# Two-tile transfers of the expert weights, with the kept results and the sample states laid out anew

## The chip, the cores and the metric

The kernel runs on one core of a Trainium2 chip. The metric is the device time of one execution in microseconds; the times below are the median and the ends of several runs. The trace is one profiled execution of the same program.

## The reference

One inference step of a two-layer decoder for 512 prompt tokens and 8 sample sequences of 4 tokens (544 rows of 1024). Each layer is a mixer and a product-key expert block (PEER):

```python
h = rmsnorm(x, g_mix); proj = h @ w_in                  # pool, q/k/v, z, beta, alpha, xq, 3 gates
y = [pool_mixer(...), gated_delta(...), mem_attend(...)]  # the delta branch carries a state per sequence
x = x + sum_n(sigmoid(gate_n) * (y_n @ w_branch[n])) @ w_o
h = rmsnorm(x, g_ffn)
s = subkeys . (h @ w_q)          # 8 heads, 2 halves, 128 keys each: top 16 of each, then top 16 of the sums
a = einsum('td,thed->the', h, take(U, idx))            # 16384 experts, 8 x 16 chosen per token
x = x + einsum('the,thed->td', softmax(best) * gelu(a), take(V, idx))
```

The outputs are the normed rows and the new pool, convolution, delta and memory states.

## The kernel before

Matrix products run as three float32r products of a high and a low part: a helper `split` (lines 94 to 96) makes the high part on ACT (`wh`, `vh`) and the low part on DVE (`wl`, `vl`), and TensorE takes high x high, high x low and low x high. Raw weight tiles come through `weights` (line 98): one ring named `wr` of three buffers of 4 KB a partition, and two buffers each for `wh` and `wl`. All of `w_mk`, `w_mv`, `w_in`, `w_branch`, `w_o`, `w_pq` and the expert table `u` go through that ring; the loads are issued on SP's queue, in program order.

A layer goes like this. **Mixer**: attention, convolution, pooling, then gates and the delta branch; `delta_sample` (line 719) reads the sample states in four loads of eight sequences (`S0`, two buffers of 4 KB), once for the products and once more to update and store them. **out_proj** (line 322) multiplies by `w_o` in eight tiles for token groups 2, 3, 4 and again in eight for groups 0, 1. **scores** (line 1215) finds the key scores, and loads the first eight expert tiles ahead into buffers of their own (`pre`, PRE = 8). **The G stage** (`second_stage`, `make_g`) turns, for the first 384 tokens (ND), the chosen experts and gates into a dense map of one-hot products; it is work of DVE. Beside it `spend` puts, by estimated costs, dense expert tiles on TensorE (`a_tile`: one tile of `u`, 24 products of 384 columns; 72 tiles before the G stage ends) and gathered rows for the other 160 tokens (`gather`: an indirect DMA of 128 rows on POOL's queue into one of four buffers `g_r`, then one DVE operation, `g_junk` or `g_acc`). The results of the first 24 dense tiles stay in SBUF in `kept` (36 KB a partition), the others go to DRAM (`ad`). **The v loop** (line 1053 on) runs 128 steps; a step multiplies one column tile of the gated results with one tile of `v` (`vr`, ring of three buffers of 4 KB, line 1096; 18 products of 512 columns), and between the steps the remaining 56 tiles of `u` and 200 gathered rows are placed. At steps 20, 24 and 28 the residual rows `xmid` are loaded into a buffer of the same `vr` ring (line 1122) and added on TensorE by the identity.

The program is written in this order, but a list scheduler with a timeline model sets the final order of each engine's and each queue's instructions. SBUF is handed out from two ends: pools open on the left unless `side="right"`. `hx`, the mixer's input and later its merged result, lies on the right; `pre` and then the gather's pool `gp` use the same right end once `hx` is closed after out_proj. `kept` lies in the pool `pe` on the left for the whole expert block.

Of the kernel before, what the change touches and what calls it, by code (L numbers as in the profile page):

```python
# [9 lines left out]
F32 = mybir.dt.float32  # L10
# [7 lines left out]
P = 128  # L18
L = 2
# [6 lines left out]
NB = 8  # L26
# [50 lines left out]
class Body:  # L77
# [20 lines left out]
    def weights(self, src, n=1024, wr=None):  # L98
        nc = self.nc
        if wr is None:  # L100
            wr = self.wp.tile([P, 1024], F32, name="wr", bufs=3)
            nc.sync.dma_start(wr[:, :n], src)
        wh = self.wp.tile([P, 1024], F32R, name="wh", bufs=2)
        wl = self.wp.tile([P, 1024], F32R, name="wl", bufs=2)
        self.split(wh[:, :n], wl[:, :n], wr[:, :n])
        return wh, wl
# [612 lines left out]
    def delta_sample(self, l, dl):  # L719
        nc, a = self.nc, self.a  # L720

        def state(h):
            S0 = dl.tile([P, NB, P], F32, name="S0", bufs=2)
            nc.sync.dma_start(S0, a["state_delta"][l, :, h * NB:(h + 1) * NB])
            return S0
# [9 lines left out]
        for g in range(32):  # L735
            if g % NB == 0:
                S0 = state(g // NB)
            nc.tensor.matmul(ps[:, g], S0[:, g % NB], wq[:, g], start=True, stop=True)
# [18 lines left out]
        for c in range(8):  # L757
            h = c // 2
            if c % 2 == 0:
                S0 = state(h)  # L760
            p = self.bank(1).rearrange("p (b e) -> p b e", b=4)
            for j in range(4):
                b = (c % 2) * 4 + j
                nc.tensor.matmul(p[:, j], kdm[h * 32:(h + 1) * 32, b], vn[h * 32:(h + 1) * 32], start=True, stop=True)
            for j in range(4):
                b = (c % 2) * 4 + j
                g = c * 4 + j
                nc.vector.scalar_tensor_tensor(S0[:, b], S0[:, b], r["egr"][:, 0, g * 4 + 3:g * 4 + 4], p[:, j],
                                               op0=OP.mult, op1=OP.add)
            if c % 2 == 1:  # L770
                nc.sync.dma_start(a["ndelta_s"][l, :, h * NB:(h + 1) * NB], S0)
# [141 lines left out]
    def a_fetch(self):  # L913
        k = self.a_next
        self.a_w = self.weights(self.a["u"][self.a_l, k], wr=self.pre.pop(k, None)) if k < NKEY else None
# [44 lines left out]
    def peer(self, l):  # L960
# [7 lines left out]
        with ExitStack() as es:  # L968
# [6 lines left out]
            self.kept = pe.tile([P, KJ, ND], F32, name="kept")  # L975
# [7 lines left out]
            with ExitStack() as es2:  # L983
# [27 lines left out]
                self.hxs.close()  # L1011
                sc = self.pool("sc", es2)
                pp = self.pool("pre", es2, side="right")
                self.pre = {k: pp.tile([P, D], F32, name=f"pre{k}") for k in range(PRE)}
# [3 lines left out]
                while self.pre:  # L1018
                    self.a_early(len(self.pre) > 1)
# [17 lines left out]
            with ExitStack() as es2:  # L1037
# [23 lines left out]
                def out(i, x, parts):  # L1061
# [3 lines left out]
                    if l + 1 < L:  # L1065
                        self.mixer_in(ns, i, parts, g, 0, h)
                        if x is None:
                            x = acc[1] if i == 4 else dv.tile([P, D], F32, name="vr", bufs=3)
                            x = x[:np_]
                            for s, p in enumerate(parts):  # L1070
                                nc.scalar.copy(x[:, s * 512:(s + 1) * 512], p)
# [4 lines left out]
                for q in order:  # L1076
# [8 lines left out]
                    for jj in range(GA):  # L1085
# [10 lines left out]
                        vr = dv.tile([P, D], F32, name="vr", bufs=3)  # L1096
                        nc.sync.dma_start(vr, a["v"][l].rearrange("(i j) d -> j i d", j=P)[j])
# [22 lines left out]
                        if step % 4 == 0 and XAT <= step < XAT + 4 * (ND // P):  # L1120
                            i = (step - XAT) // 4
                            x = dv.tile([P, D], F32, name="vr", bufs=3)
# [10 lines left out]
                        if step == NKEY - RDONE + 1:  # L1133
                            for _ in self.rows_due:
                                pass
                            ge.close()
                            if l + 1 < L:
# [78 lines left out]
    def scores(self, l, sc, val, idx, bh, bl):  # L1216
# [4 lines left out]
        for h in range(PH):  # L1221
            if h % 4 == 0:
                ssm = sc.tile([P, 2, NKEY], F32, name="ssm", bufs=2)
            for k in list(self.pre)[h * PRE // PH:(h + 1) * PRE // PH]:
# [158 lines left out]
def _layout(inp):  # L1383
# [34 lines left out]
    o["u"] = np.ascontiguousarray(u.transpose(0, 2, 4, 3, 1)).reshape(L, P, P, NK * P)  # L1418
# [82 lines left out]
```

## Time and profile before

| | us |
|---|---|
| runs shown: median (lowest, highest) of 3 | 4025.16 (4023.65, 4027.57) |
| the profiled execution's own time | 4027.84 |
| its span in the trace | 4026.0 |
| TensorE (PE) busy | 3878.3 (96%) |
| VectorE (DVE) busy | 2950.2 (73%) |
| ScalarE (ACT) busy | 1603.4 (40%) |
| mean granted TensorE clock | 0.978 |

The span is what the trace covers; the profiled execution's own time is 1.84 us longer. PE's busy time is the union of matmuls whose ends are modelled, so a full PE is not by itself PE at its peak; the issue distance between matmuls in the chain tells more. The two layers repeat the same pattern at a distance of some 1980 us.

### The profile page before, as it was taken

The page shows a single profiled execution, that of the slowest core. Times are in us where ns is not written, and L with a number is a line of the kernel's source. Part 1 is how long each engine was busy: PE and PEld are TensorE (multiplying, and loading weights), DVE is VectorE, ACT ScalarE, POOL GpSimd, SP SyncE. Part 2 cuts the span into 40 slices and gives each one's busy share as a digit, 9 for nine tenths or more (in the row PEclk, how much of TensorE's full clock was granted, in tenths as well). Part 3 has the DMA queues.
Part 4 walks back from the last instruction along what each step waited for, and adds up shares of the span by engine and source line. Part 5 has one row for each costly group of instructions (what it writes and reads, how often), then busy time and mean ns, then how long its engine had stood idle before and what let it go on. Part 6 is the DMA issues. An engine that isn't in the chain of part 4 may idle for free.

```text
span 4026.0 us, 63148 instructions
## 1 busy us (share of the span) xinstructions
PE 3878.3 (96%) x24116; PEld 3522.3 (87%) x24116; DVE 2950.2 (73%) x5811; ACT 1603.4 (40%) x2373; POOL 1038.8 (26%) x880
## 2 busy tenths in 40 slices
PE   8999999999997999999999999999999889999998
PEld 7899997898996888888888999889989778888887
DVE  5544445789998888888855444467999978888887
ACT  4532333334554333333444333343355543333333
POOL 0110110003323444443401111000034434444443
PEclk9999999999997999999999999999999889999999
DMA  7233114427888999999933322162378899999996
GB/s 261 82 124 120 54 59 149 169 64 243 302 314 317 336 344 345 337 339 339 339 111 117 125 83 67 48 235 86 101 270 302 321 335 332 346 341 342 347 333 238
DMA packets 318272, 917.60 MB, mean 228 GB/s; under 512 B 28400, under 2 KB 109680, under 8 KB 314640
## 3 DMA queue, kind: packets, MB, share of 16 engines
q1 hardware_dynamic: 218896, 518.21, 38.0%
q0 software_dynamic: 92160, 335.59, 23.2%
q10 hardware_dynamic: 6912, 59.77, 3.7%
q8 instruction: 189, 3.10, 0.3%
q14 instruction: 115, 0.94, 0.1%
HBM read 826.19 MB, written 87.26 MB: 227 GB/s over the span
## 4 chain that ended last, share of the span: by engine, by line
PE 85%; DVE 8%; issue 3%; DMA 2%; ACT 2%; POOL 1%; DVEq 0%; POOLq 0%; SPq 0%; ACTq 0%
PE mm L115 31%; PE mm L1113 17%; PE sm L115 12%; PE sm L1113 9%; PE mm L341 2%; DVE wl L96 2%; DMA g_r<-u_rows,g_e 2%; DVE g_junk L1182 1%; PE sm L628 1%; PE sm L616 1%; PE sm L904 1%; PE sm L622 1%; PE sm L885 1%; DVE ohl L1363 1%; PE sm L522 1%
## 5 line engine op out<-in xcount | busy, mean ns | idle before, releaser
L95 ACT CAST wh<-wr 128x1024 fp32r<-128x1024 f32 (+1 forms) x464 | 466.9, 1006 | 1042.8 <-PE mm L115 676.0
L96 DVE TENSOR_TENSOR wl<-wr,wh 128x1024 fp32r<-128x1024 f32 (+1 forms) x464 | 543.3, 1171 | 384.2 <-ACT wh L95 383.5
L1197 POOL DMA_INDIRECT g_r<-u_rows,g_e x320 | 459.4, 1436 | 1374.3 <-DVE g_junk L1182 654.3
L1197 POOL DMA_INDIRECT g_r<-v,g_e x320 | 449.3, 1404 | 553.7 <-DVE g_acc L1190 511.1
L115 PE MATMUL mm<-ah,wh 128*128 128x384 f32 (+1 forms) x1408 | 467.5, 332 | 19.3 <-ACT ga L934 12.6
L115 PE MATMUL mm<-ah,wl 128*128 128x384 f32 (+1 forms) x1408 | 464.2, 332 | 15.0 <-DVE wl L96 14.7
L115 PE MATMUL mm<-al,wh 128*128 128x384 f32 (+1 forms) x1408 | 461.7, 328 | 0.5 <-DVE al L96 0.5
L1190 DVE SCALAR_TENSOR_TENSOR g_acc<-g_r,g_w,g_acc 128x1024 f32<-128x1024 f32 x320 | 409.7, 1280 | 12.3 <-DMA g_r<-v,g_e 10.3
L1182 DVE SCALAR_TENSOR_TENSOR g_junk<-g_r,h2t 128x1024 f16<-128x1024 f32 x320 | 390.0, 1219 | 30.3 <-DMA g_r<-u_rows,g_e 28.9
L96 DVE TENSOR_TENSOR vl<-vr,vh 128x1024 fp32r<-128x1024 f32 x256 | 312.3, 1221 | 38.7 <-ACT vh L95 38.3
L115 PE MATMUL mm<-hh,wh 128*128 128x272 f32 x1536 | 335.4, 295 | 0.2 <-ACT hh L95 0.2
L115 PE MATMUL mm<-hh,wl 128*128 128x272 f32 x1536 | 334.3, 295 | 0.0
L115 PE MATMUL mm<-hl,wh 128*128 128x272 f32 x1536 | 328.0, 293 | 0.0
L1113 PE MATMUL mm<-vl,gwh 128*128 128x512 f32 x1024 | 316.9, 390 | 0.0
L1113 PE MATMUL mm<-vh,gwl 128*128 128x512 f32 x1024 | 316.1, 390 | 0.0
L115 PE MATMUL sm<-ah,wl 128*128 128x384 f32 x896 | 303.5, 339 | 5.9 <-DVE wl L96 5.9
L1113 PE MATMUL mm<-vh,gwh 128*128 128x512 f32 x1024 | 304.1, 392 | 2.2 <-ACT vh L95 2.2
L115 PE MATMUL sm<-ah,wh 128*128 128x384 f32 x896 | 304.7, 340 | 0.7 <-ACT stage L1372 0.7
L115 PE MATMUL sm<-al,wh 128*128 128x384 f32 x896 | 303.6, 339 | 0.0
L115 PEld LDWEIGHTS mm<-ah,wh 128*128 128x128 f32 x1408 | 267.8, 190 | 28.2 <-ACT ga L934 18.8
L115 PEld LDWEIGHTS mm<-ah,wl 128*128 128x128 f32 x1408 | 267.6, 190 | 24.0 <-DVE wl L96 23.7
L95 ACT CAST vh<-vr 128x1024 fp32r<-128x1024 f32 x256 | 269.1, 1053 | 12.1 <-DMA vr<-v 11.4
(436 smaller groups left out, 8133.7 us busy)
## 6 DMA issues: line engine op xcount, KB each, us to landing
vr<-v SPq DMA_DIRECT2D x256, 512.0 KB, 6.9
wr<-u SPq DMA_DIRECT2D x240, 512.0 KB, 6.1
wr<-w_in SPq DMA_DIRECT2D x96, 512.0 KB, 3.6
gd<-stage ACTq DMA_DIRECT2D x24, 1664.0 KB, 8.5
gt<-gd SPq DMA_DIRECT2D x52, 768.0 KB, 10.7
ad<-ga ACTq DMA_DIRECT2D x24, 768.0 KB, 6.4
gr<-ad SPq DMA_DIRECT2D x24, 768.0 KB, 8.3
wr<-w_o SPq DMA_DIRECT2D x32, 512.0 KB, 3.8
```

Source lines behind the costliest of these rows:

```text
L95: self.nc.scalar.copy(hi, src)
L96: self.nc.vector.tensor_sub(lo, src, hi.bitcast(F32))
L115: nc.tensor.matmul(o, w[:, k * P:(k + 1) * P], x[part][:, k], start=(q == 0), stop=(q == 3 * nk - 1))
L341: nc.tensor.matmul(ps[i][s][:np_], m[:, k, c], w[:, s * 512:(s + 1) * 512], start=(k == 0 and q == 0), stop=(k == NK - 1 and q == 2))
L522: nc.tensor.matmul(ps[i], x[:, k, i * P:(i + 1) * P], w[:, kk * BW:(kk + 1) * BW], start=(k == 0 and q == 0), stop=(k == NK - 1 and q == 2))
L616: nc.tensor.matmul(p[:, h], ats[:, h], dm[:, h], start=True, stop=True)
L622: nc.tensor.matmul(p[:, h], dtm[:, h], xm[:, h], start=True, stop=True)
L628: nc.tensor.matmul(p[:, h], xm[:, h], dtm[:, h], start=True, stop=True)
L1113: ins = nc.tensor.matmul(po[i][s], w[:, i * P:(i + 1) * P], v[:, s * 512:(s + 1) * 512], start=(step == 1 and m == 0), stop=(step == NKEY ...
L1182: ins = nc.vector.scalar_tensor_tensor(jk, r, 1.0, h2t[t], op0=OP.mult, op1=OP.mult, accum_out=w[:, s:s + 1])
L1190: nc.vector.scalar_tensor_tensor(acc[t], r, w[:, s:s + 1], acc[t], op0=OP.mult, op1=OP.add)
L1197: nc.gpsimd.indirect_dma_start(out=r, out_offset=None, in_=a["v" if which else "u_rows"].rearrange("l e d -> (l e) d"), in_offset=bass.Ind ...
```

## The change

Three things are done. (1) The host stores two tiles of `u` side by side; a load brings a pair, 8 KB a partition, into a ring `wr` of two buffers of 8 KB in place of three of 4 KB. Other weights still load one tile, into the first half of such a buffer. The `v` tiles are also loaded in pairs, into a ring `vr` of two buffers of 8 KB, which the `xmid` rows share; `pre` becomes four pairs. (2) `kept` is opened on the right end after out_proj, below `pre` and `gp`, and closed near the end of the v loop. (3) The sample states come in pieces of four sequences, with three buffers of 2 KB, and are stored in such pieces.

```diff
     def weights(self, src, n=1024, wr=None):
-            wr = self.wp.tile([P, 1024], F32, name="wr", bufs=3)
+            wr = self.wp.tile([P, 2048], F32, name="wr", bufs=2)
...
-        def state(h):
-            S0 = dl.tile([P, NB, P], F32, name="S0", bufs=2)
-            nc.sync.dma_start(S0, a["state_delta"][l, :, h * NB:(h + 1) * NB])
+        def state(c):
+            S0 = dl.tile([P, 4, P], F32, name="S0", bufs=3)
+            nc.sync.dma_start(S0, a["state_delta"][l, :, c * 4:(c + 1) * 4])
...
-            if c % 2 == 0:
-                S0 = state(h)
+            S0 = state(c)
...
-            if c % 2 == 1:
-                nc.sync.dma_start(a["ndelta_s"][l, :, h * NB:(h + 1) * NB], S0)
+            nc.sync.dma_start(a["ndelta_s"][l, :, c * 4:(c + 1) * 4], S0)
...
     def a_fetch(self):
         k = self.a_next
-        self.a_w = self.weights(self.a["u"][self.a_l, k], wr=self.pre.pop(k, None)) if k < NKEY else None
+        if k == NKEY:
+            self.a_w = None
+            return
+        if k % 2 == 0:
+            self.a_pair = self.pre.pop(k // 2, None)
+            if self.a_pair is None:
+                self.a_pair = self.wp.tile([P, 2048], F32, name="wr", bufs=2)
+                self.nc.sync.dma_start(self.a_pair, self.a["u"][self.a_l, k // 2])
+        self.a_w = self.weights(None, wr=self.a_pair[:, k % 2 * D:(k % 2 + 1) * D])
...
-            self.kept = pe.tile([P, KJ, ND], F32, name="kept")
...
                 self.hxs.close()
+                ke = ExitStack()
+                self.kept = self.pool("kept", ke, side="right").tile([P, KJ, ND], F32, name="kept")
                 sc = self.pool("sc", es2)
                 pp = self.pool("pre", es2, side="right")
-                self.pre = {k: pp.tile([P, D], F32, name=f"pre{k}") for k in range(PRE)}
+                self.pre = {k: pp.tile([P, 2 * D], F32, name=f"pre{k}") for k in range(PRE // 2)}
...
-                        vr = dv.tile([P, D], F32, name="vr", bufs=3)
-                        nc.sync.dma_start(vr, a["v"][l].rearrange("(i j) d -> j i d", j=P)[j])
+                        if jj % 2 == 0:
+                            vp = dv.tile([P, 2 * D], F32, name="vr", bufs=2)
+                            nc.sync.dma_start(vp, a["v"][l].rearrange("(i j n) d -> j i (n d)", j=P // 2, n=2)[j // 2])
+                        vr = vp[:, jj % 2 * D:(jj % 2 + 1) * D]
...
-                            x = dv.tile([P, D], F32, name="vr", bufs=3)
+                            x = dv.tile([P, 2 * D], F32, name="vr", bufs=2)[:, :D]
                             nc.sync.dma_start(x, self.xmid[l][i])
...
                             ge.close()
+                            ke.close()
```

The new sizes and places also move instructions. Two places on SP's queue matter below.

The first is out_proj in layer 0. In the changed program SP's queue reads there (`w_branch`, `w_o` and `w_pq` are weights, `sg` a gate read back, `pre` the expert pairs loaded ahead):

```order
L102 DMA wr<-w_o 128x1024 x2
L1235 DMA pre_7218<-u 128x2048
L1235 DMA pre_7219<-u 128x2048
L1235 DMA pre_7220<-u 128x2048
L1235 DMA pre_7221<-u 128x2048
L102 DMA wr<-w_o 128x1024 x7
L349 DMA xmid_80<-x_o 128x1024 x2
```

and before the same loads stood after the last `w_o` tile and three tiles of `w_pq`:

```order
L102 DMA wr<-w_pq 128x1024 x3
L1225 DMA pre_7195<-u 128x1024
L1225 DMA pre_7196<-u 128x1024
L349 DMA xmid_80<-x_o 128x1024
L1225 DMA pre_7197<-u 128x1024
L1225 DMA pre_7198<-u 128x1024
L349 DMA xmid_80<-x_o 128x1024
L1225 DMA pre_7199<-u 128x1024
```

So the four pairs, 4 MB, have moved ahead of the last twelve `w_o` tiles: `pre` no longer lies where `hx` is still read. Layer 1 has the same order.

The second place is the part of the v loop in which the `xmid` rows use a `vr` buffer. In the changed program SP's queue reads there, with what each row waits for:

```order
L1132 DMA vr<-xmid_80 128x1024 [waits DMAHW4_49,DMAHW2_49,DVE_49]
L1105 DMA vr<-v 128x2048 [waits DMAHW5_49,DMAHW3_49,DVE_49]
L1105 DMA vr<-v 128x2048 [waits DMAHW4_49,PE_49]
L1132 DMA vr<-xmid_80 128x1024 [waits DMAHW5_49,DVE_49]
L920 DMA wr<-u 128x2048 [waits DVE_49,Activation_49]
```

and before:

```order
L1123 DMA vr<-xmid_80 128x1024 [waits DMAHW2_49,DVE_49]
L1097 DMA vr<-v 128x1024 [waits DMAHW3_49,DVE_49]
L1097 DMA vr<-v 128x1024 [waits DMAHW4_49,DVE_49]
L1097 DMA vr<-v 128x1024 [waits DMAHW6_49,DVE_49]
L102 DMA wr<-u 128x1024 [waits DVE_49]
L1097 DMA vr<-v 128x1024 [waits DMAHW5_49,PE_49]
```

The row that waits for PE reuses the buffer of the `xmid` rows. Before, three tiles of `v` stood between the two; now one pair does.

## Rows read from the trace of the kernel before

**Rows 1.** The page's first part, PE: busy, share, instructions.
```profile
PE 3878.3 (96%) x24116; PEld 3522.3 (87%) x24116; DVE 2950.2 (73%) x5811; ACT 1603.4 (40%) x2373; POOL 1038.8 (26%) x880
```

**Rows 2.** Windows of layer 0: length, engines busy (instructions), granted clock, DMA share, GB/s.
```profile
0.00:80.00 80.00, 62.19 (x381) 54.90 (x382) 47.18 (x83) 42.74 (x71) 0.49 (x8) 0.98 0.72 247
80.00:640.00 560.00, 552.22 (x4294) 519.03 (x4293) 258.76 (x554) 199.69 (x330) 63.42 (x113) 0.99 0.29 94
640.00:720.00 80.00, 79.30 (x432) 63.94 (x431) 52.86 (x80) 33.18 (x48) 0.00 (x0) 1.00 0.66 218
...
850.00:1260.00 410.00, 370.89 (x2476) 352.33 (x2475) 403.87 (x937) 213.88 (x275) 115.33 (x79) 0.93 0.73 257
...
1310.00:2000.00 690.00, 688.90 (x3278) 600.57 (x3277) 573.16 (x688) 252.16 (x343) 303.66 (x222) 1.00 0.95 339
```

**Rows 3.** Waits of PE, 850 to 1320 us and 1300 to 2000 us: total, times, longest.
```profile
PE sm L1369 <- DVE ohh L1362: 18.4, 13, 2.8
...
PE mm L1113 <- ACT vh L95: 1.1, 1, 1.1
```

**Rows 4.** The chain in order of time: start, length, what.
```profile
77.54 24.21 PE mm L115 x192
...
1500.61 4.19 PE sm L115 x24
1512.99 4.19 PE sm L115 x24
```

**Rows 5.** Waits of SP's queue over the whole span.
```profile
SPq L102 <- DVE wl L96: 1804.8, 363, 56.0
```

**Rows 6.** DMA issues of the whole span: KB each, median us from issue to landing.
```profile
wr<-w_in SPq DMA_DIRECT2D x96, 512.0 KB, 3.6
...
sub<-subk SPq DMA_DIRECT2D x2, 1024.0 KB, 11.5
...
wr<-w_mk SPq DMA_DIRECT2D x8, 512.0 KB, 5.0
wr<-w_mv SPq DMA_DIRECT2D x8, 512.0 KB, 3.5
```

**Rows 7.** DMA issues in the G stage of layer 0, 850 to 1260 us.
```profile
wr<-u SPq DMA_DIRECT2D x66, 512.0 KB, 5.0
...
g_r<-u_rows,g_e POOLq DMA_INDIRECT x78, 6.2
```

**Rows 8.** DMA issues in the v loop of layer 0, 1310 to 2000 us.
```profile
vr<-v SPq DMA_DIRECT2D x119, 512.0 KB, 6.8
...
gt<-gd SPq DMA_DIRECT2D x23, 768.0 KB, 9.5
...
g_r<-v,g_e POOLq DMA_INDIRECT x154, 7.8
```

**Rows 9.** ACT's timeline (two rows), then DVE's, in the memory projections of layer 1.
```profile
57.79 1.05 ACT L95 CAST wh<-wr 128x1024 fp32r<-128x1024 f32 x1 [4.58 <-PE sm L115]
60.62 1.05 ACT L95 CAST wh<-wr 128x1024 fp32r<-128x1024 f32 x1 [1.51 <-PE sm L115]
...
58.87 1.23 DVE L96 TENSOR_TENSOR wl<-wr,wh 128x1024 fp32r<-128x1024 f32 x1 [4.94 <-ACT wh L95]
```

**Rows 10.** ACT's timeline in out_proj of layer 0, and SP's queue after it.
```profile
661.08 1.05 ACT L95 CAST wh<-wr 128x1024 fp32r<-128x1024 f32 x1 [0.88 <-PE mm L115]
...
677.98 1.05 ACT L95 CAST wh<-wr 128x1024 fp32r<-128x1024 f32 x1 [3.14 <-PE mm L341]
...
720.24 0.80 SPq L1225 DMA_DIRECT2D pre<-u  x2
```

**Rows 11.** PE's timeline in the v loop: the identity products of the first `xmid` rows.
```profile
1396.39 1.88 PE L1125 MATMUL mm<-vr,kc 128*128 128x512 f32 x4
```

**Rows 12.** Waits of DVE for gathered rows, 850 to 1320 us and 2850 to 3320 us.
```profile
DVE g_junk L1182 <- DMA g_r<-u_rows,g_e: 10.1, 7, 3.7
...
DVE g_junk L1182 <- DMA g_r<-u_rows,g_e: 12.3, 10, 3.0
```

More of the change, by code (lines that the diff above doesn't have):

```diff
@@ L735, in delta_sample @@
         for g in range(32):
-            if g % NB == 0:
-                S0 = state(g // NB)
-            nc.tensor.matmul(ps[:, g], S0[:, g % NB], wq[:, g], start=True, stop=True)
+            if g % 4 == 0:
+                S0 = state(g // 4)
+            nc.tensor.matmul(ps[:, g], S0[:, g % 4], wq[:, g], start=True, stop=True)
         vnT = dl.tile([P, P], F32, name="s_vnT")
@@ L765, in delta_sample @@
             for j in range(4):
-                b = (c % 2) * 4 + j
                 g = c * 4 + j
-                nc.vector.scalar_tensor_tensor(S0[:, b], S0[:, b], r["egr"][:, 0, g * 4 + 3:g * 4 + 4], p[:, j],
+                nc.vector.scalar_tensor_tensor(S0[:, j], S0[:, j], r["egr"][:, 0, g * 4 + 3:g * 4 + 4], p[:, j],
                                                op0=OP.mult, op1=OP.add)
-            if c % 2 == 1:
-                nc.sync.dma_start(a["ndelta_s"][l, :, h * NB:(h + 1) * NB], S0)
+            nc.sync.dma_start(a["ndelta_s"][l, :, c * 4:(c + 1) * 4], S0)
     def pool_part(self, l, pp, ypool):
@@ L1017, in peer @@
                 self.second_stage(sp, val[:, 24:], idx[:, 24:], last)
-                while self.pre:
-                    self.a_early(len(self.pre) > 1)
+                while self.a_next < PRE:
+                    self.a_early(self.a_next < PRE - 1)
             with ExitStack() as es2:
@@ L1067, in out @@
                         if x is None:
-                            x = acc[1] if i == 4 else dv.tile([P, D], F32, name="vr", bufs=3)
+                            x = acc[1] if i == 4 else dv.tile([P, 2 * D], F32, name="vr", bufs=2)[:, :D]
                             x = x[:np_]
@@ L1223, in scores @@
                 ssm = sc.tile([P, 2, NKEY], F32, name="ssm", bufs=2)
-            for k in list(self.pre)[h * PRE // PH:(h + 1) * PRE // PH]:
+            for k in list(self.pre)[h * PRE // 2 // PH:(h + 1) * PRE // 2 // PH]:
                 nc.sync.dma_start(self.pre[k], a["u"][l, k])
@@ L1417, in _layout @@
     u = f["peer_u"].reshape(L, P, P, NK, P)
-    o["u"] = np.ascontiguousarray(u.transpose(0, 2, 4, 3, 1)).reshape(L, P, P, NK * P)
+    u = u.transpose(0, 2, 4, 3, 1).reshape(L, P // 2, 2, P, NK * P)
+    o["u"] = np.ascontiguousarray(u.transpose(0, 1, 3, 2, 4)).reshape(L, P // 2, P, 2 * NK * P)
     o["v"] = f["peer_v"]
```

## The prediction

> **What bounds the kernel now.** I read the page's first part, then the windows cut at the stages, then the waits of PE, then the chain, and last the transfers. PE is busy for 96% of the span, DVE for 73% [rows 1], but that mean hides two kinds of stage [rows 2]. In the mixer (80 to 640 us) PE is busy 552 of 560 us and DMA 0.29. In the v loop (1310 to 2000 us) PE is busy 688.9 of 690, DMA 0.95 at 339 GB/s, and in that stretch PE waited once, for 1.1 us [rows 3]. That this is PE's real pace is seen in the chain [rows 4]: 24 products of 384 columns take 4.19 us, and the next such tile starts 12.38 us later, so the 36 products of 512 columns between them take 8.19 us, 0.2275 us each. 128 steps of 18 such products are 524 us, its 56 dense tiles at 4.19 us another 235: 759 us, about 5.9 us a step, and that is the whole of the loop. Nothing that makes a transfer cheaper can shorten it; only a stall can lengthen it. Between the two, in the G stage (850 to 1260 us), DVE is busy 403.9 of 410 us: DVE is the bound, PE loses 39 us there and that costs nothing by itself (its largest wait is for DVE's one-hot products, 18.4 us [rows 3]). The loads are early everywhere: SP's queue stood 1805 us waiting for a `wr` buffer to be released [rows 5]. So what the change can give is DVE's waits for data in the G stage and little else, and what it can take is the lead of the loads.
>
> **Part by part.** The work of PE, DVE and ACT is the same: the same splits, products and gathered rows in nearly the same order. SP issues 232 transfers fewer (120 and 8 of `u`, 128 of `v` less, 24 of the states more); SP waits most of the time, so this gives 0.
>
> *The ring `wr`, two deep.* A buffer is released when its low part is done, and its next load must land before PE wants it, now two tile times later and not three. From start of cast to end of subtraction is 57.79 to 60.10 us, 2.31 us [rows 9]. With a landing of 3.6 us (`w_in` [rows 6]) a buffer goes round in 5.9 us. A `w_in` tile takes PE 24.21 / 4 = 6.05 us [rows 4], two of them 12.1 us: hidden, with 6 us to spare; if SP's queue is held by another wait for longer than that, it shows (0 to 8 us over all). In the memory projections the casts come 2.83 us apart, at PE's pace [rows 9]. There the buffer goes round in 2.31 + 3.5 = 5.81 us for `w_mv` and 2.31 + 5.0 = 7.31 for `w_mk` [rows 6], per two tiles, so 2.90 and 3.65 us a tile: 8 x 0.07 + 8 x 0.82 = 7 us more at most. The 5.0 is a median that holds the crowded start, and PE has transposes to fill gaps with, so I take 4, between 0 and 13 (16 tiles at 0.82).
>
> *Expert pairs in the G stage.* 66 tiles in 410 us [rows 2, 7] are 6.2 us a tile. The first tile of a pair is wanted three tile times after its buffer was released, as before with three single buffers: 18.6 us, against 11.5 us for the only 1 MB load on the page [rows 6]. Hidden; were it not, DVE would wait with PE.
>
> *`v` pairs in the steady loop.* Again three steps of lead, 5.9 us each, 17.8 us. A pair has no row. 512 KB land in 6.8 us and 768 KB in 9.5 us [rows 8]; the same 2.7 us more gives 12.2 us as an estimate for 1 MB, and with the split 14.5 us. Hidden by 3.3 us, no more.
>
> *The `xmid` rows in the `vr` ring.* They hold one of two buffers, where it was one of three. The pair after such a row can only be loaded when the pair before it is split, which is two steps ahead of PE: 2 x 5.9 us and the identity products, 1.88 us [rows 11], are 13.7 us of cover for 14.5 us of need. Short by 0.8 us, say 1, three times a layer in two layers: 6 us. With a landing of 9.5 us [rows 8] it is 0; with twice 6.8 us and one more 512 KB ahead of it at 339 GB/s, 15.1 us and with the split 17.4, it is 3.7 us each, 22 in all.
>
> *`kept` on the right.* It adds no instruction, and its first write comes long after out_proj. What it moves is `pre`: the four pairs now stand on SP's queue behind the fourth `w_o` tile. Before, they were issued at 720 us, after out_proj [rows 10]. The fourth tile's load goes out when the second is split, at about 663.4 us (its cast starts at 661.08 [rows 10], and 1.05 and 1.23 us follow [rows 9]). Behind it stand 4.2 MB; 4.7 MB at 339 GB/s [rows 2] take 13.9 us, to 677.3. The fifth tile comes after that, 2 us for its own completion (3.5 us for a landing whose bytes take 1.5) and 1.05 for the cast: 680.4. PE wants it when it is through with the fourth, at 677.98, where ACT was let go for the sixth [rows 10]. About 2 us of stall a layer, 4 in all; 0 if the pairs are held back or the queue is quicker, 20 if the transfers only reach the 218 GB/s of this stage [rows 2].
>
> *The sample states.* Twice as many transfers of half the size, three in flight for two; PE has projections to run beside them in the mixer's stage, so 0, bounds 0 and 6 us.
>
> **The sum**: 4 + 6 + 4 = 14 us. The profiled execution's own time is 4027.84 us, 2.68 us above the median of the runs shown; 4027.84 + 14 - 2.68 = 4039 us.
>
> **Rivals.** *The cover holds (same).* Every term above is a few microseconds short of cover by estimated landings; if pairs land in 9.5 us and the burst of `pre` is held back until later, they are 0 to 4 in all and the time stays at 4025 to 4030. For it: before, PE waited only 1.1 us in a loop whose DMA share was 0.95 [rows 2, 3]. Against it: two of the three covers are thinner than a quarter of what they must hide.
>
> *Shorter waits for gathered rows (faster).* In the G stage DVE is the bound, so its waits for data count in full: 10.1 us in layer 0 and 12.3 in layer 1 are for gathered rows [rows 12]. Fewer and larger transfers beside them could make the rows land sooner. If two thirds go, 15 us, and the covers hold, the time is 4025 - 15 = 4010 us; this decides if rows then land well under the 6.2 us of the G stage [rows 7]. The Trainium skill, DMA: Bandwidth & Descriptors, section Bandwidth, speaks for this case: transfers should be batched to 1 MB or more, below which much of the peak is lost. The trace doesn't bear it out as a total: with 512 KB loads, several in flight, the v loop already moves 339 GB/s [rows 2].
>
> *Pairs get in the way of gathered rows (much slower).* The opposite on the same spot: a gathered row that meets a pair in the DMA engines may have to let 1 MB pass and not 512 KB, 1.5 us more at 339 GB/s. There are 33 pairs in the G stage of a layer [rows 7]. A row has four buffers of lead, and on average 410 / 78 = 5.3 us a row [rows 2, 7] leaves it enough; near the end and in the first steps of the loop two rows follow each other. If a quarter of the 66 pairs cost their 1.5 us, it is 25 us beyond the sum: 4064 us. The Trainium skill, the same page, section Queues, rings and completion order, speaks for this: an engine goes round the queues by whole packets, draining one before it turns to the next. The landing of gathered rows, 7.8 us in the loop [rows 8], is what to compare.
>
> That the change doesn't do what it says can be left out: the changed program's SP queue has the 1 MB loads.
>
> **Numbers.** Forecast case (the thinner leads cost 8 to 32 us): 0.45. Cover holds: 0.27. Faster: 0.18. Much slower: 0.10. A measurement of this kernel can tell about 0.2%, 8 us, from no change: below 4017 is faster, above 4033 slower. That gives slower 0.55, same 0.27, faster 0.18. The range of 4010 to 4075 holds the first two cases, the faster one down to its price, and the slower one up to 11 us above its price, which the upper bounds of the terms (13, 22, 20 us) could also reach; what is left out is a full gain of the row waits or several upper bounds at once.
>
> **What would show it.** Right: in the v loop PE's waits rise from 1.1 us to some 3 us, at three places near steps 20 to 28, with ACT's `vh` waiting for the DMA of `v`; in out_proj PE stands about 2 us at the fifth `w_o` tile while the `pre` pairs land; in the first 80 us ACT waits for `w_mk` loads and not for PE; the steady loop keeps its 12.38 us. Wrong: PE's waits in these places unchanged (cover holds), or a G stage that is 5 us or more shorter or longer between the first gathered row and the first product of the v loop, with DVE's waits for gathered rows changed by as much. If the mixer's stage (80 to 640 us) is longer by over 5 us, the two-deep ring cost more than I see, or the queue was held at the states.

## The result, and the profile after

The changed kernel takes 4049.23 us (median of 7 runs, 4033.47 to 4056.33) against 4025.39 us for the kernel before (7 runs beside it, 4023.65 to 4033.60): ratio 1.0051, 95% interval 1.0033 to 1.0070, slower. Forecast was 4039 us and slower with a chance of 0.55, so the sign and the range held; the time was 10 us above the forecast, and where it went is only half of what was forecast. (By the ratio the change costs 20 us, where 14 were forecast.) The profiled execution took 4056.33 us (span 4054.5), the slowest of the seven, so its stages overstate the loss. The changed kernel ran again beside the experiments (below); both profiles stand in the table, cut at the first and the last start of three groups of products: out_proj's, the one-hot products of the G stage, and those with `v`. Three executions beside the experiments, one of e2 (13331.82 us) and two of the kernel before (7322.82 and 7691.30 us), stand far off all others and do not enter the ratios.

| us, layer 0 / layer 1 | before | changed | changed, second profile |
|---|---|---|---|
| start, or end of layer 0's loop, to out_proj | 661.1 / 605.3 | 667.5 / 605.4 | 667.4 / 605.3 |
| out_proj | 59.2 / 59.2 | 66.5 / 67.5 | 68.0 / 67.7 |
| out_proj to the first G product | 276.7 / 277.6 | 271.3 / 272.2 | 271.6 / 271.1 |
| G products | 266.9 / 268.8 | 271.0 / 264.9 | 264.7 / 269.1 |
| G to the first `v` product | 28.0 / 25.8 | 31.2 / 27.5 | 29.5 / 27.0 |
| `v` loop | 743.8 / 743.2 | 744.7 / 752.7 | 740.9 / 747.7 |

The stretches of [rows 1, 2], in the changed kernel:

```profile
PE 3890.1 (96%) x24116; PEld 3521.7 (87%) x24116; DVE 2939.6 (73%) x5811; ACT 1599.6 (39%) x2371; POOL 1085.2 (27%) x880
```
```profile
0.00:80.00 80.00, 60.33 (x353) 51.56 (x354) 45.84 (x81) 39.77 (x68) 0.20 (x4) 0.98 0.68 228
80.00:640.00 560.00, 554.55 (x4298) 520.69 (x4296) 256.74 (x550) 198.54 (x329) 64.60 (x117) 0.99 0.31 98
640.00:720.00 80.00, 74.83 (x401) 60.88 (x400) 47.14 (x70) 30.27 (x45) 0.00 (x0) 0.94 0.62 216
...
1310.00:2000.00 690.00, 687.10 (x3256) 597.63 (x3255) 558.22 (x688) 249.65 (x340) 301.88 (x215) 1.00 0.92 335
```

The mixer (80 to 640 us) is as it was. The stretch with out_proj has lost 4.5 us of PE's busy time and granted clock, 1.00 to 0.94. In the loop the DMA engines now have gaps, 0.95 to 0.92. PE's waits of [rows 3], in the loops of layer 0 (1308 to 2052 us) and layer 1 (3290 to 4042 us):

```profile
PE mm L1122 <- DVE vl L96: 2.3, 2, 2.0
PE sm L1122 <- DVE vl L96: 1.0, 1, 1.0
...
PE mm L1122 <- DVE vl L96: 8.1, 5, 5.3
```

1.1 us became 3.8 and 8.1. Of those, 2.0 us stand between 1420 and 1490 us, where the `xmid` rows were forecast to be short, but the largest, 5.3 us, is in layer 1's last 100 us. In layer 0's loop ACT and DVE wait longer for data. DVE's waits for gathered rows before, then those and ACT's in the changed kernel (ACT's were 3.9 us before):

```profile
DVE g_junk L1182 <- DMA g_r<-u_rows,g_e: 2.5, 4, 1.2
DVE g_acc L1190 <- DMA g_r<-v,g_e: 1.2, 2, 0.8
```
```profile
DVE g_acc L1200 <- DMA g_r<-v,g_e: 33.2, 24, 3.6
...
DVE g_junk L1192 <- DMA g_r<-u_rows,g_e: 22.6, 10, 3.4
...
ACT vh L95 <- DMA vr<-v: 23.4, 10, 7.6
```

The transfers of [rows 8], then the waits of SP's queue in the same stretch, before and in the changed kernel:

```profile
vr<-v SPq DMA_DIRECT2D x59, 1024.0 KB, 8.2
wr<-u SPq DMA_DIRECT2D x23, 1024.0 KB, 8.4
gt<-gd SPq DMA_DIRECT2D x24, 768.0 KB, 11.7
...
g_r<-v,g_e POOLq DMA_INDIRECT x142, 8.3
```
```profile
SPq L1097 <- DVE vl L96: 336.5, 102, 6.7
SPq L1082 <- DVE gwl L96: 19.2, 8, 4.1
```
```profile
SPq L1105 <- DVE vl L96: 284.8, 44, 13.1
SPq L920 <- DVE wl L96: 90.5, 21, 13.7
SPq L1089 <- DVE gwl L96: 54.1, 8, 10.4
```

A pair lands in 8.2 us, well under the 12.2 us estimated for it. But at a `v` load SP stands 284.8 / 44 = 6.5 us on average until the buffer is free, where it was 336.5 / 102 = 3.3, and at a `gr` load (L1089, the dense results read back from DRAM) 54.1 / 8 = 6.8, where it was 2.4; all that is behind it in the queue stands too. There are half as many `v` loads, so the sum of SP's stands at them is not larger (284.8 against 336.5 us), but each is longer. Apart from stalls the loop keeps its pace; the chain has the same 12.38 us from one dense tile to the next as [rows 4]:

```profile
1625.18 4.19 PE sm L115 x24
...
1637.56 4.19 PE sm L115 x24
```

Out_proj of layer 0 on SP's queue, then on ACT, to be laid beside [rows 10]:

```profile
667.37 2.84 SPq L102 DMA_DIRECT2D wr<-w_o  x2
670.26 2.98 SPq L1235 DMA_DIRECT2D pre<-u  x4
675.22 28.84 SPq L102 DMA_DIRECT2D wr<-w_o  x7
```
```profile
676.13 1.05 ACT L95 CAST wh<-wr 128x1024 fp32r<-128x1024 f32 x1 [2.20 <-PE mm L341]
685.95 1.04 ACT L95 CAST wh<-wr 128x1024 fp32r<-128x1024 f32 x1 [8.77 <-DMA wr<-w_o]
```

PE's waits for the casts in the same stretch, of which there were none before:

```profile
PE sm L341 <- ACT wh L95: 2.7, 1, 2.7
PE mm L341 <- ACT wh L95: 1.5, 2, 1.2
```

The four pairs go out at 670 us and the fifth `w_o` tile at 675.22; its cast starts 10.7 us later. This is the place that was forecast.

### The profile page after: what moved, and what is told of

Its sections match the earlier page's. It is cut to its first block, busy times and chain, and to the rows that moved or that the text cites. A ratio compares the mean times of both kernels' runs of the same rounds, so it can differ in the third digit from the quotient of the medians.

```text
span 4054.5 us, 62556 instructions
## 1 busy us (share of the span) xinstructions
PE 3890.1 (96%) x24116; PEld 3521.7 (87%) x24116; DVE 2939.6 (73%) x5811; ACT 1599.6 (39%) x2371; POOL 1085.2 (27%) x880
## 4 chain that ended last, share of the span: by engine, by line
PE 67%; DVE 12%; DMA 10%; issue 6%; ACT 2%; POOL 2%; SPq 0%; DVEq 0%; POOLq 0%; ACTq 0%
PE mm L115 29%; PE mm L1122 11%; PE sm L115 8%; PE sm L1122 6%; DMA g_r<-u_rows,g_e 3%; DMA g_r<-v,g_e 3%; DVE wl L96 2%; DVE g_junk L1192 2%; POOL g_r L1207 2%; DMA wr<-w_o 1%; PE sm L628 1%; PE sm L616 1%; DMA vr<-v 1%; DMA gt<-gd 1%; PE sm L901 1%
## 5 line engine op out<-in xcount | busy, mean ns | idle before, releaser
L1207 POOL DMA_INDIRECT g_r<-u_rows,g_e x320 | 492.2, 1538 | 1388.9 <-DVE g_e L1175 681.1
L1207 POOL DMA_INDIRECT g_r<-v,g_e x320 | 461.7, 1443 | 542.5 <-DVE g_acc L1200 471.5
L1122 PE MATMUL mm<-vl,gwh 128*128 128x512 f32 x1024 | 319.7, 393 | 10.7 <-DVE vl L96 10.4
```

The lines of the kernel that those rows point to most:

```text
L1122: ins = nc.tensor.matmul(po[i][s], w[:, i * P:(i + 1) * P], v[:, s * 512:(s + 1) * 512], start=(step == 1 and m == 0), stop=(step == NKEY ...
L1207: nc.gpsimd.indirect_dma_start(out=r, out_offset=None, in_=a["v" if which else "u_rows"].rearrange("l e d -> (l e) d"), in_offset=bass.Ind ...
```

## The experiments

The kernels ran in three sessions. The kernel before ran beside each session and had medians of 4031.07, 4032.59 and 4030.36 us, so ratios are compared; 0.1% is 4 us. The theory to begin with: the leads of the two-deep rings, the burst of `pre` and the `v` pairs lose; nothing gains but what comes back before G.

| kernel | median us (runs) | ratio, 95% interval |
|---|---|---|
| e1 kept results alone | 4031.20 (12) | 0.9996, 0.9980 to 1.0012 |
| e2 changed, `u` single | 4043.40 (12, one of them 13331.82) | 1.0026, 1.0010 to 1.0043 |
| e3 changed, `v` single | 4034.94 (12) | 1.0003, 0.9990 to 1.0017 |
| e4 changed, `pre` held | 4036.43 (12) | 1.0008, 0.9992 to 1.0024 |
| e5 changed, again | 4045.03 (5) | 1.0037, 1.0024 to 1.0051 |
| e6 changed, singles four deep | 4036.82 (11) | 1.0010, 0.9998 to 1.0021 |
| e7 e6 and `pre` held | 4036.74 (12) | 1.0011, 1.0000 to 1.0021 |
| e8 changed, `v` pairs in halves | 4045.32 (12) | 1.0029, 1.0016 to 1.0042 |
| e9 all single, four deep | 4032.32 (12) | 1.0011, 0.9996 to 1.0025 |
| e10 e6 with `v` single, four deep | 4020.93 (12) | 0.9975, 0.9962 to 0.9989 |
| e11 changed without `xmid` rows | 4037.49 (12) | 1.0020, 1.0007 to 1.0033 |
| e12 changed, rows due earlier | 4109.55 (6) | 1.0202, 1.0177 to 1.0227 |

**The yardstick (e5).** The changed kernel, unaltered.

> The changed kernel once more, unaltered, as the yardstick beside the others. Theory (its loss is in its order of loads, not in one unlucky execution): 0.3 to 0.7% over the kernel before, out_proj at 66 us a layer, the v loop of layer 1 at 749 us or more with over 5 us of PE waits, as in its first profile. Rival (the v loop of 752.7 us was that execution's own): loop of layer 1 within 2 us of 744, total within 0.3% of the kernel before.

Ratio 1.0037; out_proj 68.0 and 67.7 us; the loop of layer 1 747.7 us with 5.6 us of PE waits, 5.3 of them in one wait in its last 100 us, as in the first profile. By the ratios the loss is 15 us here and 20 in the first session. That execution's 752.7 us were in part its own, the 5.3 us wait was not.

### Out_proj: the burst or the ring

**e1**, the kernel before with one edit:

```diff
-            self.kept = pe.tile([P, KJ, ND], F32, name="kept")
...
+                ke = ExitStack()
+                self.kept = self.pool("kept", ke, side="right").tile([P, KJ, ND], F32, name="kept")
...
+                            ke.close()
```

> The kernel before with the kept results moved to the other end alone: single tiles, three 4 KB buffers for weights and for v. Theory (the early burst of pre loads delays the fifth w_o tile by itself, whatever the ring): out_proj takes 64 to 67 us a layer instead of 58.7, gives about 5 us back before the G stage, memory projections and v loop are as before, total 4025 to 4031 us. Rival (the burst hurts only a two-deep ring): out_proj stays at 59 to 61 us, the 5 us before the G stage are gained all the same, total 4012 to 4020 us.

The move of the kept results alone brings the burst forward into out_proj, seven of its eight tiles ahead of the sixth `w_o` tile, as SP's timeline of e1 shows, and out_proj stays at 59.2 us in both layers, without a PE wait for a `w_o` tile:

```profile
667.13 2.73 SPq L102 DMA_DIRECT2D wr<-w_o  x2
669.91 3.74 SPq L1227 DMA_DIRECT2D pre<-u  x7
674.59 0.33 SPq L102 DMA_DIRECT2D wr<-w_o  x1
```

With three buffers the burst costs nothing, so the theory fell. The rival's sum fell as well: before G only 1.6 and 2.0 us were gained, and the total is that of the kernel before.

**e4**, the changed kernel with each pair of `pre` tied to a column of `q`:

```diff
-            for k in list(self.pre)[h * PRE // 2 // PH:(h + 1) * PRE // 2 // PH]:
-                nc.sync.dma_start(self.pre[k], a["u"][l, k])
             q = sc.tile([P, 2, N], F32, name="q", bufs=2)
...
+            for k in list(self.pre)[h * PRE // 2 // PH:(h + 1) * PRE // 2 // PH]:
+                nc.gpsimd.tensor_copy(self.pre[k][:, 0:1], q[:, 0, 0:1])
+                nc.sync.dma_start(self.pre[k], a["u"][l, k])
```

> The changed kernel with each pair of pre held back until scores: POOL writes one column of it from q ahead of its load. Theory (the 4 MB burst ahead of the fifth w_o tile makes out_proj long): out_proj 59 to 61 us a layer instead of 66 to 67, and the 5.4 us a layer before the G stage are given back in part, total 3 to 12 us under the changed kernel. Rival (the two-deep ring alone makes it long): out_proj stays at 64 us or more, the 5.4 us are given back, total 5 to 12 us over the changed kernel.

Out_proj 61.1 and 63.1 us: two buffers without the burst cost 2 to 4 us a layer, the burst the other 4 to 7. The stretch before G stayed at 271.9 and 271.0 us, so its gain does not come from the burst. Ratio 1.0008, some 12 us under the yardstick's (8.6 by the medians of the two sessions).

**e6**, the changed kernel with two single tiles in one 8 KB buffer, each loaded by itself:

```diff
-            wr = self.wp.tile([P, 2048], F32, name="wr", bufs=2)
+            if self.half_w is None:
+                self.half_w = self.wp.tile([P, 2048], F32, name="wr", bufs=2)
+                wr = self.half_w[:, :1024]
+            else:
+                wr, self.half_w = self.half_w[:, 1024:], None
```

> The changed kernel with two single weight tiles in each 8 KB buffer, so that singles stand up to four deep in the same space; pairs as they are. Theory (out_proj is long because the fifth w_o tile, two deep, is asked for only behind the burst of pre): with four in flight out_proj is 59 to 61 us a layer although the burst stays where it was, memory projections lose 2 to 4 us of what they had gained, the loop of layer 1 stays at 748 us or more, total 10 to 18 us under the changed kernel. Rival (the burst takes the DMA engines whatever the ring): out_proj stays at 64 us or more, total within 6 us of the changed kernel.

Out_proj 59.1 and 59.2 us with the burst where it was (issued at 670.20 us). The theory of ring and burst together holds. The total fell by 8 us (by the ratios 11), less than the 15 to 17 that the stage gave back in the two layers: the loop of layer 1 was 752.6 us in this profile, with one wait of 6.6 us at its end.

**e7**, the edits of e4 and e6 together:

```diff
+                wr, self.half_w = self.half_w[:, 1024:], None
...
+                nc.gpsimd.tensor_copy(self.pre[k][:, 0:1], q[:, 0, 0:1])
```

> Both at once: singles four deep in the 8 KB buffers, and pre held back to scores. Theory: out_proj 59 to 60 us a layer, as with the four-deep ring alone, since either would do; before the G stage no more than 2 us a layer change; total within 5 us of the run with the four-deep ring alone. Rival (each has a part of its own): out_proj another 2 us a layer shorter than with the deep ring alone, total 5 us or more under it.

Out_proj 59.2 and 59.2 us, total 0.1 us from e6: either remedy does, as the theory had it.

In the memory projections the last product starts at 76.7 us in the kernel before, at 77.4 and 77.6 with three single buffers (e1, e2), at 80.6 on average of the seven profiles with two (78.3 to 82.1). ACT waits 8.3 to 13.6 us for `w_mv` in each of those seven and in no other. Four deep (e6, e7, e9, e10) it is 76.9 to 80.8 us without that wait, so what else moves it stays open. The waits of the changed kernel:

```profile
ACT wh L95 <- DMA wr<-w_mv: 10.8, 5, 3.9
ACT wh L95 <- DMA wr<-w_mk: 3.8, 3, 2.4
```

That these microseconds reach the total is not shown. Out_proj of layer 0 began at 666.9 us in e1, whose ring has three buffers, nearly as late as in the changed kernel (667.5), and at 661.1 in e7 as in the kernel before. From 300 to 500 us PE is busy for all of the 200 us in the kernel before, in e1 and in the changed kernel, but at a granted clock of 1.00, 0.97 and 0.98; by these figures that is some 6 and 4 us (an estimate).

### The loop: `v` pairs, `u` pairs, size or buffers

**e2** and **e3** undo one kind of pair each; in e2 all singles, `u` among them, have three 4 KB buffers:

```diff
-            wr = self.wp.tile([P, 2048], F32, name="wr", bufs=2)
+            wr = self.wp.tile([P, 1024], F32, name="wr", bufs=3)
...
+        if k >= PRE:
+            self.a_w = self.weights(self.a["u"][self.a_l, k // 2][:, c])
```

> The changed kernel with u in single transfers and three 4 KB buffers for all single weights; v stays in pairs. Theory (v pairs in two buffers, landing in 8 us, are what makes the v loop late): the loop keeps about 25 us of ACT waits for DMA of v a layer and 20 to 50 us of DVE waits for gathered rows, the memory projections are as before (661.6 us to out_proj), total 4036 to 4046 us with runs that spread by over 5 us. Rival (the u pairs bring the spread and the late gathered rows): loop waits as before, 1.1 us of PE, total 4022 to 4030 us.

```diff
-                            vp = dv.tile([P, 2 * D], F32, name="vr", bufs=2)
-                            nc.sync.dma_start(vp, a["v"][l].rearrange("(i j n) d -> j i (n d)", j=P // 2, n=2)[j // 2])
-                        vr = vp[:, jj % 2 * D:(jj % 2 + 1) * D]
+                        vr = dv.tile([P, D], F32, name="vr", bufs=3)
+                        nc.sync.dma_start(vr, a["v"][l].rearrange("(i j) d -> j i d", j=P)[j])
```

> The changed kernel with v in single transfers and three 4 KB buffers; u stays in pairs and the other weights in its two buffers. Theory (v pairs make the loop late): loop back at 743 to 745 us a layer and PE waits for vl and vh under 1.5 us; the start (+6.4 us) and out_proj (+7.7 us a layer, less 5.4 before the G stage) stay, total 4034 to 4042 us with a narrow spread. Rival (u pairs do it): gathered rows stay late, 50 us and more of DVE waits in the loops, total 4045 to 4056 us.

With `v` in pairs (e2) the loop of layer 1 keeps 749.5 us and 7.0 us of PE waits; with `v` single (e3) it is 745.3 and 3.6. DVE's waits for gathered rows in the two loops are 26 and 38 us in e2, 20 and 31 in e3, 56 and 64 in the first changed profile: both kinds of pair add to them, but it is the `v` pairs that cost time, 14 us by the ratios of e3 and e5. The theory holds on that total; where in the kernel it is lost comes below. What it could not explain is e2: it has the three-deep ring back, worth 8 us or more by e6, and is only 4 us under the yardstick by the ratios. Single `u` must then lose what the ring gains (e10 below shows it).

**e8** fills each `v` buffer by two transfers of 512 KB:

```diff
-                            nc.sync.dma_start(vp, a["v"][l].rearrange("(i j n) d -> j i (n d)", j=P // 2, n=2)[j // 2])
                         vr = vp[:, jj % 2 * D:(jj % 2 + 1) * D]
+                        nc.sync.dma_start(vr, a["v"][l].rearrange("(i j) d -> j i d", j=P)[j])
```

> The changed kernel with each 8 KB buffer of v filled by two 512 KB transfers in place of one of 1 MB; the buffers, the order in which they come free and the u pairs stay. Theory (two buffers that come free only in pairs leave too little ahead): the loop of layer 1 stays at 748 to 753 us, PE waits 5 us or more and DVE waits for gathered rows 40 us or more a layer. Rival (the 1 MB transfer itself lands late and holds the gathered rows up): loop within 2 us of 745, PE waits under 3 us, waits for gathered rows 20 to 35 us as with single v, total 6 to 12 us under the changed kernel.

4045.32 us, the time of the changed kernel, and 749.6 us in layer 1's loop with 6.5 us of PE waits. The waits for gathered rows went down to 28 and 41 us, so size has a part in those, but hardly in the time: by the ratios e8 is 3 us under the yardstick, and the two intervals overlap for the most part. e8 and e3 load `v` by the same 512 KB transfers; 12 KB in three buffers that come free one by one (e3) beats 16 KB that come free in twos (e8) by 10 us, the two intervals overlapping only from 1.0016 to 1.0017. SP's mean stand at a `v` load and at a `gr` load goes the same way: 5.5 and 6.4 us in e8, 6.5 and 6.8 in the changed kernel; 3.9 and 2.6 in e3, 3.3 and 2.4 in the kernel before.

The profiles place only a part of the 14 us. In the seven with `v` in 8 KB buffers (changed, e2, e4 to e8) layer 1's loop takes 745.7 to 752.7 us, and the wait near its end is 3.6 to 6.6 us; in the five with 4 KB buffers (before, e1, e3, e9, e10) it is 742.7 to 745.3 us and 0 to 1.9. That is 6 us in the mean. Layer 0's loop is no longer with pairs (means 741.4 and 742.4 us). Over all runs the mean granted clock is 0.9774 in e5 and 0.9792 in e3, at 4040 us up to 7 us (an estimate, in part the same time). Where the rest is lost stays open.

**e9** cuts the changed kernel's two rings of 16 KB into four buffers of 4 KB; **e10** does so for `v` alone and keeps `u` in pairs, with e6's ring:

```diff
-            wr = self.wp.tile([P, 2048], F32, name="wr", bufs=2)
+            wr = self.wp.tile([P, 1024], F32, name="wr", bufs=4)
...
+                        vr = dv.tile([P, D], F32, name="vr", bufs=4)
```

> The changed kernel with the same 16 KB in each of its two rings cut into four buffers of 4 KB, filled by single transfers of 512 KB; pre, the kept results and the state pieces as in the change. Theory (the pairs lose, not the rest of the change): out_proj 59 us a layer, DVE waits for gathered rows in the v loops under 15 us a layer, loops of 742 to 745 us, total 6 to 14 us under the kernel before (out_proj to G about 2 us a layer shorter, the memory projections 2 to 4 us), so 4012 to 4022 us against 4025. Rival (kept results and states shift the order for the worse whatever the transfers): loop waits stay at 40 us or more a layer, total at or above the kernel before.

```diff
+                wr, self.half_w = self.half_w[:, 1024:], None
...
+                        vr = dv.tile([P, D], F32, name="vr", bufs=4)
```

> As the run with four buffers of 4 KB, but u in pairs of 1 MB (singles share the 8 KB buffers two by two). Theory (the u pairs have a smaller part of the loss, as the run with single v showed): DVE waits for gathered rows 20 to 31 us a layer, loop of layer 1 at 745 to 748 us, total 2 to 8 us over the run with four single buffers. Rival (only the v pairs matter once singles are four deep): waits under 15 us, total within 2 us of that run.

e9 did what the theory said in the loops (743.7 and 742.7 us; waits for rows 5 and 18 us) and in out_proj (59.2), but not in the total, 1.0011: the 5 us a layer before G were gone. e10 went against both: its waits for rows are 14 and 26 us, and yet it is 11 us (by the ratios 14) under e9 and 0.25% under the kernel before, faster than either of the two kernels of this case. So the `u` pairs gain. The stage that differs is the one from out_proj to the first G product: 274.7 to 277.6 us in the eight layers of the four profiles with single `u` (before, e1, e2, e9), 270.5 to 272.5 in the twenty layers of the ten with pairs, 5 us a layer, about 10 in all. In the mean these 5 us are still there at the first `v` product (573.2 us after out_proj with single `u`, 568.5 with pairs), but not in e10's own profile (573.4 and 573.8). The kernel before, on DVE, where the first gathered rows arrive, and on PE:

```profile
932.29 1.22 DVE L1182 SCALAR_TENSOR_TENSOR g_junk<-g_r,h2t 128x1024 f16<-128x1024 f32 x1 [2.17 <-DMA g_r<-u_rows,g_e]
...
933.44 1.22 DVE L96 TENSOR_TENSOR wl<-wr,wh 128x1024 fp32r<-128x1024 f32 x1
```
```profile
934.72 0.69 PE L115 MATMUL mm<-ah,wl 128*128 128x384 f32 x1 [2.92 <-DVE wl L96]
935.20 0.53 PE L115 MATMUL mm<-ah,wh 128*128 128x384 f32 x1
935.52 0.53 PE L115 MATMUL mm<-al,wh 128*128 128x384 f32 x1
...
941.14 0.33 PE L115 MATMUL mm<-ah,wl 128*128 128x384 f32 x1
941.31 0.33 PE L115 MATMUL mm<-ah,wh 128*128 128x384 f32 x1
```

DVE waits for a gathered row, the low part of a `u` tile stands behind it, PE waits 2.92 us for that, and then 17 products start 0.32 us apart, where they start 0.17 us apart later: 5.4 us for 2.9. Such a wait of PE for `wl`, of 2.8 to 4.3 us, stands in this stage in each of the eight layers with single `u`; in the twenty with pairs none is longer than 0.9. The windows of the kernel before and of e10 have the granted clock beside it (the column before the DMA share):

```profile
920.00:960.00 40.00, 35.07 (x184) 34.11 (x184) 36.89 (x120) 13.61 (x19) 16.97 (x12) 0.91 0.73 245
935.00:940.50 5.50, 5.50 (x18) 5.50 (x19) 5.50 (x18) 0.00 (x0) 1.63 (x2) 0.50 0.78 252
```
```profile
920.00:960.00 40.00, 37.51 (x210) 35.91 (x209) 39.18 (x137) 17.01 (x23) 17.41 (x11) 1.00 0.72 245
```

So PE's products after the stall run at the lower of the clock's two levels. Over all runs the mean granted clock is 0.9778 in e9 and 0.9798 in e10, at 4030 us up to 8 us (an estimate).

DVE's waits for these first rows are 3.0 to 4.3 us a layer in the four kernels with single `u` and 0 to 1.7 in the six with pairs that were read (changed, e3 to e6, e10). The 8 us in which the first four rows are asked for, in layer 0 of the kernel before (922 to 930 us) and of e10 (926.5 to 934.5), show what stands beside them:

```profile
wr<-u SPq DMA_DIRECT2D x1, 512.0 KB, 4.9
g_r<-u_rows,g_e POOLq DMA_INDIRECT x4, 6.0
```
```profile
g_r<-u_rows,g_e POOLq DMA_INDIRECT x4, 5.2
```

With single tiles a `u` load goes out among the rows, and they land in 6.0 us in the median (6.9 in e9); with pairs the loads fall before and behind, and the rows land in 5.2. No edit moved a load to try this, so it is read and not shown. The profiled execution of e10 took 4033.43 us, the slowest of its twelve, and so does not show its whole gain by stages.

### The terms of the forecast that were left

**e11**, the changed kernel without the three loads of `xmid` rows a layer (the expectation's "four" is a slip):

```diff
-                            x = dv.tile([P, 2 * D], F32, name="vr", bufs=2)[:, :D]
-                            nc.sync.dma_start(x, self.xmid[l][i])
+                            x = self.ident
                             for s in range(2):
-                                nc.tensor.matmul(po[i][s], self.ident, x[:, s * 512:(s + 1) * 512], start=False,
-                                                 stop=False)
+                                nc.tensor.matmul(po[i][s][:, :P], x, x, start=False, stop=False)
```

> The changed kernel without the four loads of xmid rows in the loop of v; in place of the residual a 128x128 identity product is added to each accumulator, so that part of the output is left out. Theory (the xmid rows cost little: each takes a pair's buffer once, at the steps 20 to 32 where only 0.5 to 1.2 us of PE waits stand, and the loss is at the end of the loop): total within 4 us of the changed kernel, DVE waits for gathered rows 40 us or more a layer. Rival (the forecast's term: 6 us in both layers for rows in the two-buffer ring): total 5 to 8 us under the changed kernel.

7.5 us under the changed kernel (7 by the ratios), as the rival had it, but not for its reason: the identity products left out were shorter, too. Those of layer 0 in the changed kernel, and in e11:

```profile
L1134 PE MATMUL mm<-vr,kc 128*128 128x512 f32 x8 | 3.8, 592 | 0.0
L1134 PE MATMUL sm<-vr,kc 128*128 128x512 f32 x4 | 1.9, 592 | 0.0
```
```profile
L1133 PE MATMUL mm<-kc 128*128 128x128 f32 x8 | 1.2, 274 | 0.0
L1133 PE MATMUL sm<-kc 128*128 128x128 f32 x4 | 0.6, 274 | 0.0
```

5.7 us less 1.8 is 3.9 us a layer, 7.8 in all: the whole difference. For a buffer held by the rows nothing is left, and PE's waits (4.2 and 6.2 us) and the waits for gathered rows (47 and 52 us) stayed. Where the rows were forecast to be short, some 147 us into the loop, PE waits 1.9 and 1.5 us in e11 without any such row, and never more than 2.1 at once in the kernels with them. The interval overlaps the yardstick's, so by the total alone a few us either way are not excluded.

**e12** lets the gathered rows be due earlier:

```diff
-RDONE = 6
+RDONE = 10
```

> The changed kernel with the gathered rows spread so that the last is due ten steps ahead of the loop's end instead of six. Theory (in layer 1 the loop ends late because the last weighted sums of gathered rows stand before the last splits of v on VectorE): the wait of 5 us or more for vl in the last 100 us of layer 1 goes, loop back to 742 to 746 us, total 3 to 9 us under the changed kernel. Rival (the rows are held back by the DMA engines all through the loop, so that asking earlier only moves the waits): DVE waits for gathered rows grow to over 60 us a layer, PE waits as long elsewhere in the loop, total within 2 us of the changed kernel.

2% over the kernel before and 1.6% over the yardstick; neither theory nor rival had it. The four products that take up the finished rows now stand ahead of 51 us of `v` products on PE, where they were behind them all, and PE waited for the rows, once in each layer:

```profile
2025.32 3.59 PE L1156 MATMUL sm<-g_acc,kc 128*32 128x512 f32 x4 [31.34 <-issue]
...
4043.34 3.43 PE L1156 MATMUL sm<-g_acc,kc 128*32 128x512 f32 x4 [31.18 <-DVE g_acc L1200]
```

The rows' last sum came some 727 us into the loop, against 737 in the yardstick's, though asked for 23 us earlier. So the rows cannot simply be had sooner; but as the edit moved products as well, it says nothing on the 5.3 us wait at the loop's end. In the yardstick's profile that wait is for the `vl` below, on DVE; it stands behind a weighted sum that waited 4.17 us for its gathered row:

```profile
4008.83 1.28 DVE L1200 SCALAR_TENSOR_TENSOR g_acc<-g_r,g_w,g_acc 128x1024 f32<-128x1024 f32 x1 [4.17 <-DMA g_r<-v,g_e]
...
4010.50 1.22 DVE L96 TENSOR_TENSOR vl<-vr,vh 128x1024 fp32r<-128x1024 f32 x1
```

That the late rows make the loss at the loop's end is read from this, and not shown by an edit.

## Why the prediction was right or wrong

**The loop's length.** The forecast's sum for the loop, 759 us, is 15 us more than the 743.8 that the same trace shows from the first to the last `v` product; a step is 5.8 us and not 5.9. No term hangs on the difference.

**The ring in the memory projections, 4 us: the size right, by luck.** The last product came 3.9 us later on average of seven profiles. But the forecast had nearly all of it at `w_mk` and next to nothing at `w_mv`; ACT waited 1.1 to 4.7 us for `w_mk` and 8.3 to 13.6 for `w_mv`. With singles four deep the last product was still 2.6 us later on average, and that any of it reaches the total is not shown.

**The burst in out_proj, 2 us a layer: right place, mis-sized.** The forecast had the fifth tile land 18.2 us after out_proj began (679.3 less 661.1); it landed 18.4 after (685.9 less 667.5). What failed is the step from there to PE: PE stood 2.7 us for that tile and 1.5 for two later ones, not 2, and the granted clock was 0.85 from 680 to 690 us. The stage grew by 7.3 to 8.8 us a layer in the two profiles. In the total it is 8 to 12 us (e4, e6, e7), so part of it may have been made up for later.

**The `xmid` rows, 6 us: wrong.** e11 leaves nothing for them, within its interval, and the wait at their place stays without them. The cover for the pair behind such a row was forecast to be 13.7 us against 14.5 us of need; with pairs landing in 8.2 and not 12.2 us there was no need of that size.

**`v` pairs in the steady loop, 0 because hidden by 3.3 us: wrong, the largest step.** Their landing was overestimated and their cost missed all the same: 14 us (e3 against e5; e10 against e6 the same). The step looked at a pair's own lead alone. It did not count that a buffer now comes free for two tiles at once, and that SP stands twice as long at each such load, with the loads of the other rings behind it. e8 shows that the time goes with the buffers more than with the 1 MB transfer; that it is SP's queue through which they take it is read from SP's waits, and the profiles place only the 6 us in layer 1's loop.

**`u` pairs, 0 because hidden: wrong in sign.** They gain 11 to 14 us (e10 against e9). This is the faster rival, shorter waits for gathered rows, near its price of 15 us, but not by its sum. It counted DVE's waits from 850 us to the loop, and their sum went from [rows 12] to 12.1 and 5.4 us, in one layer up; what goes with the 5 us a layer is the 3.1 and 3.6 us for the first rows, before the first G product, where DVE's waits hold PE and its clock back. The Trainium skill, DMA: Bandwidth & Descriptors, section Bandwidth, wants transfers batched to 1 MB. The runs agree for `u` in the time, though no run shows that bandwidth was the reason; for `v` they do not: the time went with the buffers more than with the size (e8).

**Pairs in the way of gathered rows, the slower rival: half seen.** In the loops DVE's waits for them rose from 4 and 13 us to 56 and 64, and e8 takes a third to a half of that away. But it does so without gaining time.

**Kept results and states.** The kept results cost nothing by themselves, as forecast: e1 is at 0.9996. The states, in all kernels from e2 on, were not tried alone.

In sum: 4 (memory projections, if they reach the total), 8 to 12 (out_proj) and 14 (`v` pairs), less 11 to 14 (`u` pairs), is 12 to 19 us; measured were 15 and 20 by the ratios, each within some 5 to 8 us. The forecast of 14 came near by luck: a missed loss and a missed gain were of one size.

## What to carry to other kernels

Before tiles are joined into larger transfers, count for each ring the buffers that come free one by one: at the same SBUF, four single tiles of `v` beat two pairs (e10 against e6), in a loop where one in-order queue feeds several rings. It is no rule for all rings: pairs of `u` beat four singles (e10 against e9). Price a burst that is brought forward by the ring that it delays, and a stall of PE by the slower products behind it too. A change with several parts can hide a gain inside a loss, so undo the parts one at a time, and in pairs.

## What the runs showed that was not expected

- A stall of 2.92 us on PE cost about 5.4: the 17 products behind it started 0.32 us apart and not 0.17, with a granted clock of 0.50 from 935.0 to 940.5 us, where it was 1.00 before the stall. 384 columns in 0.32 us are 1.2 a ns: the lower of the clock's two levels, 1.2 GHz.
- A 1 MB pair landed in 8.2 us where 512 KB took 6.8 [rows 8], with the DMA engines 92% busy.
- One edit to the place of a tile that no instruction of out_proj touches (e1) moved eight loads by 50 us, from 720 to 670 us.
- Runs of one kernel spread over 20 to 30 us in these sessions (e10 4013.75 to 4033.43, the kernel before 4018.74 to 4048.12 beside it), as much as the whole change or more, and the mean granted clock goes with it: 0.980 and 0.975 in those two runs of the kernel before. A profile is one draw of that, and e10's happened to be its slowest.
